# Two attention stages of an encoder kernel: issue order of the score passes, of the value products, and a wider key product

## The chip, the cores and the metric

The kernel runs on one core of a Trainium2 chip. The metric is the device time of one execution in microseconds, from the first to the last instruction. Three executions of the kernel before took 863.78, 861.42 and 863.94 us, median 863.78 us.

## The reference, cut to what matters

A two-layer encoder with 256 tokens and 1024 features, batch one. Layer 0 mixes tokens with a long convolution on 512 channels beside a latent attention of 8 heads; layer 1 mixes them with a differential attention of 8 heads. Each layer then has a cross-attention into 256 memory tokens and a squared-ReLU MLP. The parts that the change touches:

```python
# latent attention, layer 0: 8 heads, 64 plain + 32 rotary key features, 64 value features
kv = (rms_norm(ckv, kv_norm) @ w_ukv).reshape(B, S, 8, 64 + 64)
k_nope, vv = jnp.split(kv, [64], axis=-1)
kf = concat([k_nope, broadcast(k_pe)], axis=-1)              # 96 features per head
o_mla = softmax(qf @ kf.T * 96 ** -0.5) @ vv                 # per head

# differential attention, layer 1: 16 maps of 64 features, two per head
p = softmax(q @ k.T * 64 ** -0.5).reshape(B, 8, 2, 256, 256)
o = (p[:, :, 0] - lam * p[:, :, 1]) @ v                      # per head
```

## The kernel before, in words

All activations of the 256 tokens stay in SBUF as two tiles of 128 tokens; weights stream in through one DMA queue (SP), 512 KB at a time, in the order of issue. Where full precision is wanted, each operand is split into a high and a low part of type fp32r (ScalarE rounds the high part at L105 or L100, VectorE subtracts for the low part at L106 or L101), and a product is three matmuls into one PSUM place: high times high, high times low, low times high. That is the helper `mm3`; its three matmuls have lines L110, L111 and L112, whoever calls it, so the profile tells its callers apart by the tiles. Other products, those of the latent attention's scores (L562) and values (L570) among them, are plain fp32 matmuls; the trace shows each of these as two passes, which is why 16 value products have 32 rows.

PSUM has three pools of banks: four of tag `h`, three of tag `b` (`wk()`), one of tag `f`. Working tiles of 512 columns in SBUF have the tag `t2`, with four buffers in layer 0. The profile leaves the numbers of buffers and parameters out: `b`, `t`, `qkT` and `in_hy_w_dram` stand for all of their kind.

The stages are issued in an order written out by hand (`ORDER_EVEN`, `ORDER_ODD`), as source code. The framework's planner then settles, at build time, the order of instructions on each engine: it takes instructions that its own estimate finds ready, earlier source first, and hands a buffer to a tile when one is free. So an instruction whose PSUM bank is not free is passed by later ones, and the order on the chip is not that of the source. On the chip each engine then follows its own list, and waits where an operand is late.

The places that the change touches:

- `keys_values` (L532 to L545). The weight `w_ukv` has, per head, 64 columns for keys and then 64 for values. For each pair of heads one `b` bank is taken, and each head's keys are one `mm3` with 64 stationary columns, so the result sits on partitions 0 to 63, 256 columns per head: 8 heads make 24 matmuls of 256 columns. ScalarE copies each pair out in one copy of 64 x 512 (L539). The values of all heads are one `mm3` per token tile, which reads every second block of 64 columns of the weight.
- `mla_out` and `mla_o` (L565 to L583). For one head the softmaxed scores are transposed (L426), copied to SBUF (L428) and multiplied by the values (L570): two matmuls of 64 stationary columns and 256 moving columns, accumulated over the two key tiles. An even head writes partitions 0 to 63 of a bank, the odd head after it partitions 64 to 127 of the same bank; the bank is taken at the even head and held until the odd head is done, when L105 and L106 split it into `catm`.
- `od_a` (L798 to L822). A head of the differential attention has two maps. Their queries and keys sit on partitions 0 to 63 and 64 to 127 of one tile, so each score product uses 64 rows of the array. For each of two query tiles and each map there is one `mm3`; the two maps write two `b` banks. In the source all three passes of map 0 come ahead of the three of map 1, and then the second query tile follows in the same way.
- `_layout` (L957) hands `w_ukv` over as it is.

The order of the layer-0 stages around them: queries (U), keys and values (K), transposed queries (R), scores and softmax of head n (Sn), value products of head n (On), chunks of the convolution's input projection (Hn), filters (Fn, whose second weight is loaded into a `t2` tile at L350), and the two spectra (P0, P1), long chains of VectorE work.

Of the kernel before, what the change touches and what calls it, by code (L numbers as in the profile page):

```python
# [17 lines left out]
P = 128  # L18
# [9 lines left out]
PI_LO = 3.1415925  # L28
# Order in which the stages are issued: a letter names the stage (see the run() calls), digits are its arguments.
ORDER_EVEN = "N G J L H0 U K R S0 D H1 F0 S1 T0 S2 S3 P0 O0 O1 O2 H2 S4 O3 H3 T1 F1 S5 S6 O4 O5 Y S7 H4 P1 H5 O6 O7 M W"  # L30
# [8 lines left out]
def tile_encoder(ctx: ExitStack, tc: tile.TileContext, a: dict, out: bass.AP):  # L39
    nc = tc.nc  # L40
# [19 lines left out]
    def wk():  # L60
        return T(ps, [P, 512], F32, "b", bufs=3)
# [10 lines left out]
    def t2(n=512, dt=F32):  # L72
        return T(cur["pool"], [P, 512], dt, "t2", bufs=cur["n2"])[:, :n]
# [10 lines left out]
    def v3(t, k):  # L84
        return t.rearrange("p (k n) -> p k n", k=k)
# [22 lines left out]
    def mm3(o, l, r, first, last):  # L108
        (lh, ll), (rh, rl) = l, r
        nc.tensor.matmul(o, lh, rh, start=first, stop=False)  # L110
        nc.tensor.matmul(o, lh, rl, start=False, stop=False)  # L111
        nc.tensor.matmul(o, ll, rh, start=False, stop=last)  # L112

    def run(order, **ops):
        for w in order.split():
            ops[w[0]](*(int(n) for n in w[1:]))

# [1 line left out]
    es = ExitStack()  # L119
# [43 lines left out]

# [1 line left out]
    def rstd_of(ssq, n, dim, eps):  # L165
# [48 lines left out]

# [1 line left out]
    def proj_x(h, half, k0, nk, n, banks, first, last):  # L216
# [59 lines left out]

# [1 line left out]
    memT = [v3(T(cst, [P, 2048], F32R, f"memT{i}"), 8) for i in range(2)]  # L278
# [21 lines left out]

# [1 line left out]
    def sin_of(b, bias, dst):  # L302
# [96 lines left out]

# [1 line left out]
    def softmax_e(sc, scale=None):  # L401
# [29 lines left out]

    # ======== even mixer ========
    h = v3(t8(F32R), 8), v3(t8(F32R), 8)
# [27 lines left out]
    kT = v3(t8(), 8)  # L461
# [70 lines left out]
    def keys_values():  # L532
        wh, wl = weight(a["w_ukv"])
        for u in range(4):
            b = wk()
            for c in range(2):
                sl = (slice(None), slice((2 * u + c) * P, (2 * u + c) * P + 64))
                mm3(b[:64, c * 256:(c + 1) * 256], (wh[sl], wl[sl]), (latT[0][:, 2, :], latT[1][:, 2, :]), True, True)
            nc.scalar.copy(kT[:64, 2 * u:2 * u + 2, :], v3(b[:64, :], 2))  # L539
        for t in range(2):  # L540
            b = wk()
            sl = (slice(None), 2, slice(t * P, (t + 1) * P))
            wv = [z.rearrange("p (h d) -> p h d", d=P)[:, :, 64:] for z in (wh, wl)]
            mm3(b, (latT[0][sl], latT[1][sl]), wv, True, True)
            nc.scalar.copy(vl[t], b)  # L545
# [18 lines left out]

    def mla_out(hd, e3, ob):  # L565
        pT = v3(t2(), 2)
        transposed(e3, pT)
        r0 = 64 * (hd % 2)
        for m in range(2):
            nc.tensor.matmul(ob[r0:r0 + 64, :256], vl[m][:, hd * 64:(hd + 1) * 64], pT[:, m, :], start=m == 0, stop=m == 1)  # L570

    sc_ = {}
# [4 lines left out]
    def mla_o(hd):  # L577
        if hd % 2 == 0:
            sc_["b"] = wk()
        mla_out(hd, sc_[hd], sc_["b"])  # L580
        if hd % 2:
            split(catm[0][:, hd // 2, :], catm[1][:, hd // 2, :], sc_["b"][:, :256])

# [53 lines left out]

    # ======== cross-attention and MLP ========
    def cross(l, cur_):
# [94 lines left out]

    # ======== odd mixer ========
    os_ = ExitStack()
# [61 lines left out]
    def od_a(hd):  # L798
        j, c = divmod(hd, 4)
        q, k = qkT[0, hd // 2], qkT[1, hd // 2]  # L800
        c %= 2
        av = t2()
        a3 = v3(av, 2)
        es_, su = [], []
        bs = [wk(), wk()]
        for t in range(2):
            for m in range(2):
                rows = slice(64 * m, 64 * m + 64)
                mm3(bs[m][:, t * 256:(t + 1) * 256], [z[rows, c, t * P:(t + 1) * P] for z in q], [z[rows, c, :] for z in k],
                    True, True)  # L810
        for b in bs:
            e3, s_ = softmax_e(b)
            es_.append(e3)
            su.append(s_)
        w = col(2)
        nc.vector.reciprocal(w, su[1])
        nc.vector.scalar_tensor_tensor(w, w, nlam, su[0], op0=ALU.mult, op1=ALU.mult)
        eps = T(op, [P, 2], F32, "eps", bufs=4)
        nc.vector.scalar_tensor_tensor(eps, su[0], SUBLN_EPS, su[0], op0=ALU.mult, op1=ALU.mult)
        for t in range(2):  # L820
            nc.vector.scalar_tensor_tensor(a3[:, t, :], es_[1][:, t, :], w[:, t:t + 1], es_[0][:, t, :],
                                           op0=ALU.mult, op1=ALU.add)  # L822
        st[hd] = a3, eps
# [105 lines left out]
def _layout(i, c):  # L929
# [11 lines left out]
    def both(fn, w):  # L941
# [14 lines left out]
        "w_uq": i["mla_w_uq"][0].reshape(2, P, 768),  # L956
        "w_ukv": i["mla_w_ukv"][0],  # L957
        "w_out_ev": rows(i["ev_w_out"][0]),
# [45 lines left out]
```

## Time and profile before

| | |
|---|---|
| median of three runs | 863.78 us (861.42 to 863.94) |
| profiled execution | 861.42 us, which is its span (861.4 us on the page) |
| TensorE matmul busy | 841.5 us (98%) |
| VectorE / ScalarE busy | 567.4 us (66%) / 482.8 us (56%) |
| DMA | 139.53 MB, mean 162 GB/s |
| score passes of the differential attention (`qkT`) | 96 matmuls, 485.6 to 559.6 us |
| value products of the latent attention (L570) | 32 passes, 67.1 to 122.0 us |
| keys of the latent attention (L110 to L112, `latT` by 64 columns) | 24 matmuls, from 37.4 us |

How to read the views: the page has one execution. A row of the timeline gives the start in us, the duration in us, engine, line, operation, tiles and shapes, how many instructions were merged, and, in brackets, idle time ahead of it with what ended it. The duration of a matmul is its way through the array, and successive matmuls overlap; what one costs is the distance from its start to the next start. "128*64 128x256" means 128 rows and 64 columns of the array in use, 256 columns streamed. The table of windows gives, per stretch, the busy time of each engine with the count of its instructions in brackets, the granted TensorE clock, the DMA share and GB/s.

### The profile page before, as it was taken

How to read it: one execution, taken by the hardware profiler on the slowest of the kernel's cores; microseconds unless marked ns; L12 is line 12 of the kernel's file. 1: busy time of each engine (PE TensorE's matmuls, PEld its weight loads, DVE VectorE, ACT ScalarE, POOL GpSimd, SP SyncE). 2: the span in 40 equal slices, each digit the busy share in tenths (PEclk: the TensorE clock that was granted, in tenths of full speed). 3: DMA queues.
4: the chain of work that ended last, by engine and by line, in shares of the span. 5: the costliest groups of instructions: out<-in, count | busy, mean ns of one | idle time of the engine just before them, and what ended most of it. 6: DMA issues, size and time to landing. Idle time of an engine off the chain costs nothing.

```text
span 861.4 us, 13548 instructions
## 1 busy us (share of the span) xinstructions
PE 841.5 (98%) x5326; PEld 742.0 (86%) x5326; DVE 567.4 (66%) x880; ACT 482.8 (56%) x784; POOL 21.4 (2%) x54
## 2 busy tenths in 40 slices
PE   6999999999999999999999999999999999999996
PEld 4967587999989999999988787789998999999995
DVE  5878986855557655655568889576564765565553
ACT  5864444755447555555467676675443755555542
POOL 0100000000000000000000010200000000000000
PEclk9999999999999999999999999999999999999998
DMA  7550317744344555555536524325432465555531
GB/s 259 201 216 18 118 43 276 259 157 154 117 147 173 195 189 183 191 191 182 191 126 222 171 99 155 139 99 196 149 121 74 167 201 181 187 195 183 185 121 49
DMA packets 39526, 139.53 MB, mean 162 GB/s; under 512 B 4515, under 2 KB 5283, under 8 KB 39462
## 3 DMA queue, kind: packets, MB, share of 16 engines
q1 hardware_dynamic: 39462, 138.66, 46.8%
q8 instruction: 42, 0.69, 0.3%
q14 instruction: 22, 0.18, 0.1%
HBM read 137.59 MB, written 1.05 MB: 161 GB/s over the span
## 4 chain that ended last, share of the span: by engine, by line
PE 86%; issue 7%; DMA 2%; ACT 2%; DVE 1%; POOL 1%; SPq 0%; POOLq 0%; ACTq 0%
PE h L110 14%; PE h L111 14%; PE h L112 14%; PE b L110 11%; PE b L111 10%; PE b L112 10%; PE f L110 2%; PE f L111 2%; PE f L112 2%; PE b L175 1%; DMA t<-in_hy_w_dram 1%; DMA pack<-in_pack_dram 1%; PE b L839 1%; PE b L426 1%; DMA wraw<-in_xa_wk_dram 1%
## 5 line engine op out<-in xcount | busy, mean ns | idle before, releaser
L106 DVE TENSOR_TENSOR wlo<-wraw,whi 128x1024 fp32r<-128x1024 f32 (+2 forms) x131 | 158.5, 1213 | 120.7 <-ACT whi L105 119.9
L105 ACT CAST whi<-wraw 128x1024 fp32r<-128x1024 f32 (+2 forms) x131 | 135.7, 1041 | 146.9 <-PE b L111 58.0
L100 ACT ACTIVATE whi<-wraw,zero,cpack 128x512 fp32r<-128x512 f32 x208 | 159.3, 809 | 66.9 <-PE b L111 33.3
L101 DVE SCALAR_TENSOR_TENSOR wlo<-wraw,cpack,whi 128x512 fp32r<-128x512 f32 x208 | 150.6, 750 | 54.5 <-ACT whi L100 54.2
L110 PE MATMUL b<-t,whi 128*128 128x256 f32 x544 | 154.3, 284 | 0.0
L112 PE MATMUL b<-t,wlo 128*128 128x256 f32 x544 | 154.1, 283 | 0.0
L111 PE MATMUL b<-t,whi 128*128 128x256 f32 x544 | 154.1, 283 | 0.0
L110 PEld LDWEIGHTS b<-t,whi 128*128 128x128 f32 x544 | 104.5, 192 | 0.9 <-issue 0.4
L111 PEld LDWEIGHTS b<-t,whi 128*128 128x128 f32 x544 | 104.5, 192 | 0.5
L112 PEld LDWEIGHTS b<-t,wlo 128*128 128x128 f32 x544 | 104.5, 192 | 0.0
L112 PE MATMUL h<-whi,ul 128*128 128x512 f32 x256 | 100.0, 390 | 0.0
L111 PE MATMUL h<-wlo,uh 128*128 128x512 f32 x256 | 99.9, 390 | 0.0
L110 PE MATMUL h<-whi,uh 128*128 128x512 f32 x256 | 99.9, 390 | 0.0
L110 PE MATMUL h<-whi,t 128*128 128x512 f32 x192 | 77.1, 402 | 0.0
L111 PE MATMUL h<-wlo,t 128*128 128x512 f32 x192 | 76.6, 399 | 0.0
L112 PE MATMUL h<-whi,t 128*128 128x512 f32 x192 | 76.0, 398 | 0.0
L112 PEld LDWEIGHTS h<-whi,ul 128*128 128x128 f32 x256 | 48.1, 188 | 9.9
L110 PE MATMUL h<-t,whi 128*128 128x256 f32 x192 | 55.8, 291 | 0.6 <-ACT t L105 0.6
L110 PEld LDWEIGHTS h<-whi,uh 128*128 128x128 f32 x256 | 48.2, 188 | 9.5
L111 PEld LDWEIGHTS h<-wlo,uh 128*128 128x128 f32 x256 | 48.1, 188 | 9.5
L111 PE MATMUL h<-t,whi 128*128 128x256 f32 x192 | 55.3, 288 | 1.0 <-DVE t L106 1.0
L112 PE MATMUL h<-t,wlo 128*128 128x256 f32 x192 | 55.4, 289 | 0.0
(287 smaller groups left out, 1549.2 us busy)
## 6 DMA issues: line engine op xcount, KB each, us to landing
wraw<-in_mlp_up_dram SPq DMA_DIRECT2D x64, 512.0 KB, 3.3
wraw<-in_mlp_down_dram SPq DMA_DIRECT2D x64, 512.0 KB, 3.2
wraw<-in_od_w_qkv_dram SPq DMA_DIRECT2D x24, 512.0 KB, 4.3
wraw<-in_xa_wq_dram SPq DMA_DIRECT2D x16, 512.0 KB, 4.3
wraw<-in_xa_wo_dram SPq DMA_DIRECT2D x16, 512.0 KB, 3.6
wraw<-in_w_hy_dram SPq DMA_DIRECT2D x12, 512.0 KB, 4.6
wraw<-in_w_out_ev_dram SPq DMA_DIRECT2D x8, 512.0 KB, 4.8
wraw<-in_xa_wv_dram SPq DMA_DIRECT2D x8, 512.0 KB, 4.9
```

Of the source, the lines that this page charges most:

```text
L100: nc.scalar.activation(h_, r_, AF.Identity, bias=zero, scale=g)
L101: nc.vector.scalar_tensor_tensor(l_, r_, g, h_.bitcast(F32), op0=ALU.mult, op1=ALU.subtract)
L105: nc.scalar.copy(hi, src)
L106: nc.vector.tensor_tensor(lo, src, hi.bitcast(F32), op=ALU.subtract)
L110: nc.tensor.matmul(o, lh, rh, start=first, stop=False)
L111: nc.tensor.matmul(o, lh, rl, start=False, stop=False)
L112: nc.tensor.matmul(o, ll, rh, start=False, stop=last)
L175: nc.tensor.transpose(b[:, k * P:(k + 1) * P], x[:, k * P:(k + 1) * P], ident)
L426: nc.tensor.transpose(b3[:, m, t * P:(t + 1) * P], p3[:, t, m * P:(m + 1) * P], ident)
L839: nc.tensor.matmul(ob[:, t * P:(t + 1) * P], aT[:, m, t * P:(t + 1) * P], vo[j][:, m, c * P:(c + 1) * P], start=m == 0, stop=m == 1)
```

## The change

Three edits. The score passes of a head's two maps alternate pass by pass through a new helper `abreast`. The value products of two heads move from the even and the odd head's step to the odd head's step, and alternate between the heads; the even head's transposed block waits in its `t2` tile, and the bank is taken only then. The columns of `w_ukv` are put on the host's side into key columns of all heads, then value columns of all heads, so that keys of two heads are one `mm3` of 128 stationary columns; ScalarE copies each head's keys out by itself, the second head's from partitions 64 to 127 to partitions 0 to 63.

```diff
+    def abreast(jobs):
+        for i, (il, ir) in enumerate(((0, 0), (0, 1), (1, 0))):
+            for o, l, r in jobs:
+                nc.tensor.matmul(o, l[il], r[ir], start=i == 0, stop=i == 2)
...
         for u in range(4):
             b = wk()
+            mm3(b[:, :256], [z[:, u * P:(u + 1) * P] for z in (wh, wl)], [z[:, 2, :] for z in latT], True, True)
             for c in range(2):
-                sl = (slice(None), slice((2 * u + c) * P, (2 * u + c) * P + 64))
-                mm3(b[:64, c * 256:(c + 1) * 256], (wh[sl], wl[sl]), (latT[0][:, 2, :], latT[1][:, 2, :]), True, True)
-            nc.scalar.copy(kT[:64, 2 * u:2 * u + 2, :], v3(b[:64, :], 2))
+                nc.scalar.copy(kT[:64, 2 * u + c, :], b[64 * c:64 * c + 64, :256])
...
-            wv = [z.rearrange("p (h d) -> p h d", d=P)[:, :, 64:] for z in (wh, wl)]
-            mm3(b, (latT[0][sl], latT[1][sl]), wv, True, True)
+            mm3(b, (latT[0][sl], latT[1][sl]), (wh[:, 512:], wl[:, 512:]), True, True)
...
-    def mla_out(hd, e3, ob):
-        pT = v3(t2(), 2)
-        transposed(e3, pT)
-        r0 = 64 * (hd % 2)
-        for m in range(2):
-            nc.tensor.matmul(ob[r0:r0 + 64, :256], vl[m][:, hd * 64:(hd + 1) * 64], pT[:, m, :], start=m == 0, stop=m == 1)
...
     def mla_o(hd):
-        if hd % 2 == 0:
-            sc_["b"] = wk()
-        mla_out(hd, sc_[hd], sc_["b"])
+        pT = v3(t2(), 2)
+        transposed(sc_[hd], pT)
+        sc_[hd] = pT
         if hd % 2:
-            split(catm[0][:, hd // 2, :], catm[1][:, hd // 2, :], sc_["b"][:, :256])
+            ob = wk()
+            for m in range(2):
+                for c in range(2):
+                    h_ = hd - 1 + c
+                    nc.tensor.matmul(ob[64 * c:64 * c + 64, :256], vl[m][:, h_ * 64:(h_ + 1) * 64], sc_[h_][:, m, :],
+                                     start=m == 0, stop=m == 1)
+            split(catm[0][:, hd // 2, :], catm[1][:, hd // 2, :], ob[:, :256])
...
         for t in range(2):
-            for m in range(2):
-                rows = slice(64 * m, 64 * m + 64)
-                mm3(bs[m][:, t * 256:(t + 1) * 256], [z[rows, c, t * P:(t + 1) * P] for z in q], [z[rows, c, :] for z in k],
-                    True, True)
+            abreast([(bs[m][:, t * 256:(t + 1) * 256],
+                      [z[64 * m:64 * m + 64, c, t * P:(t + 1) * P] for z in q],
+                      [z[64 * m:64 * m + 64, c, :] for z in k]) for m in range(2)])
...
-        "w_ukv": i["mla_w_ukv"][0],
+        "w_ukv": i["mla_w_ukv"][0].reshape(P, 8, 2, 64).transpose(0, 2, 1, 3).reshape(P, 1024),
```

## The prediction, made before the run

> **What bounds the kernel now.** I read the page first, then the windows around the three edits, then the timeline of each. The page:
>
> ```profile
> span 861.4 us, 13548 instructions
> ...
> PE 86%; issue 7%; DMA 2%; ACT 2%; DVE 1%; POOL 1%; SPq 0%; POOLq 0%; ACTq 0%
> ```
>
> TensorE makes 86% of the chain that ended last. So time saved on TensorE counts where nothing else is just as late. The windows (keys; the stretch after them; the stretch of the value products, and two further on that come up below):
>
> ```profile
> 37.40:40.30 2.90, 2.90 (x26) 2.71 (x24) 2.50 (x8) 2.90 (x6) 0.00 (x0) 1.00 0.90 285
> 40.30:44.00 3.70, 3.70 (x27) 3.02 (x25) 3.10 (x4) 3.70 (x8) 0.00 (x0) 1.00 0.62 228
> ```
> ```profile
> 66.00:126.00 60.00, 59.59 (x357) 44.59 (x356) 53.11 (x114) 27.27 (x55) 0.74 (x2) 1.00 0.15 49
> 165.00:172.00 7.00, 5.38 (x38) 4.98 (x38) 5.43 (x6) 3.63 (x5) 0.00 (x0) 0.91 0.93 333
> 172.00:180.00 8.00, 8.00 (x61) 8.00 (x60) 2.92 (x3) 3.17 (x4) 0.00 (x0) 0.87 0.52 168
> ```
>
> After the length of the window come TensorE, weight loads, VectorE, ScalarE, GpSimd, the granted TensorE clock, the DMA share. Around the keys ScalarE has no idle time either (2.90 of 2.90 us, 3.70 of 3.70); around the value products VectorE comes second, 53.11 of 60 us.
>
> **Part 1, keys.** It removes 12 of 24 matmuls and replaces four ScalarE copies by eight of half the width.
>
> ```profile
> 37.43 0.28 PE L110 MATMUL b<-latT,whi 128*64 128x256 f32 x1
> 37.55 0.28 PE L111 MATMUL b<-latT,whi 128*64 128x256 f32 x1
> ```
> ```profile
> 38.95 1.54 ACT L539 COPY t<-b 64x512 f32<-64x512 f32 x3
> 40.38 1.06 ACT L105 CAST whi<-wraw 128x1024 fp32r<-128x1024 f32 x1
> 41.34 0.59 ACT L539 COPY t<-b 64x512 f32<-64x512 f32 x1
> ```
> ```profile
> 42.14 1.93 PE b L554 x16
> 44.07 0.23 SPq L142
> 44.30 0.05 issue
> 44.36 7.16 DMA t<-in_hy_w_dram
> 51.51 0.14 issue
> 51.65 3.67 PE h L356 x8
> ```
>
> One matmul of 256 columns costs 0.12 us (37.43 to 37.55), so TensorE saves 12 x 0.12 = 1.4 us. I count it as nothing. ScalarE works without a break from 37.40 to 44.00 (the windows), so its four key copies (1.54 + 0.59 = 2.1 us) and the cast between them set when banks come free for the values and for the transposes L554; eight copies of half the width cost no less. And the chain of waits, the fence above, shows what stands behind: the transposes L554 release a load on SP (L142), the filter weight is issued behind it at 44.36 and lands at 51.51, and L356 starts at 51.65. TensorE arriving earlier waits there longer. The bounds: -1.4 us if ScalarE and the load follow; +2.0 us if each narrow copy takes as long as a wide one (1.54 / 3 = 0.51 us, eight of them 4.1 us) and the load moves back as much. A copy's width must count for something, so I stay between them, at nothing. The values' contiguous read changes no count of columns: nothing.
>
> **Part 2, value products.** The timeline around the first head's, and four other fp32 passes in the chain of waits:
>
> ```profile
> 66.85 0.28 PE L110 MATMUL h<-t,whi 128*128 128x256 f32 x1
> 67.06 1.08 PE L570 MATMUL b<-t,vl 128*64 128x256 f32 x4
> 68.07 0.44 PE L426 MATMUL b<-cpack,t 128*128 128x128 f32 x2
> ```
> ```profile
> 55.32 0.86 PE b L562 x4
> ```
>
> A head's product is four passes, 67.06 to 68.07: 1.01 us. Four plain fp32 passes of 256 columns without such a change of shape cost 0.86 (L562), so 0.15 us of it is extra, and the matmul ahead takes 0.21 (66.85 to 67.06) instead of 0.12: 0.09 more. A visit to the 64-column shape thus costs 0.24 us besides its passes; a head costs 1.10, eight heads 8.8 us.
>
> After the change there are four visits, of eight passes each, and neighbours use the two column halves. Two bounds. No overlap: 4 x (8 x 0.215 + 0.24) = 7.8, a saving of 1.0 us. Full overlap, each half going its own way: 4 x (0.86 + 0.24) = 4.4, a saving of 4.4 us. No row of before has both column halves side by side. The nearest are the two row halves of the score passes:
>
> ```profile
> 523.96 0.39 PE L112 MATMUL h<-whi,t 128*128 128x512 f32 x1
> 524.19 0.40 PE L110 MATMUL h<-whi,t 128*128 128x512 f32 x1
> 524.52 0.38 PE L110 MATMUL b<-qkT,qkT 64*128 64x256 f32 x1
> ...
> 525.09 0.28 PE L111 MATMUL b<-qkT,qkT 64*128 64x256 f32 x2
> 525.21 0.28 PE L112 MATMUL b<-qkT,qkT 64*128 64x256 f32 x2
> ```
>
> There two passes (x2) start every 0.12 us, the time of one, so row halves overlap fully. They also pay the same kind of toll on entering: 0.33 us from 524.19 to 524.52 where the 512-column matmul ahead took 0.23, so 0.10 more, against 0.09 for the value products. That toll shows that the value products already run in a half-array shape; the keys, also 64 columns wide, pay none (37.43 to 37.55), and their halves are never neighbours. So I take the end that these rows are nearest to, full overlap, 4.4 us gross. Were each product's two passes to stay in a row, a pair would need five steps instead of four and 0.9 us of it would be lost; the score passes above, which pair out of source order, speak for four.
>
> How much of it arrives? VectorE is the cover that runs out. Its second spectrum ends just when TensorE wants it:
>
> ```profile
> 101.02 1.02 PE L378 MATMUL h<-z,c_dft 128*128 128x512 f32 x2
> 102.40 1.08 PE L570 MATMUL b<-t,vl 128*64 128x256 f32 x4 [0.35 <-ACT t L428]
> ```
> ```profile
> 119.68 0.68 DVE L397 TENSOR_TENSOR h<-h,h 128x512 f32<-128x512 f32 x1
> ```
> ```profile
> 120.28 0.39 PE L624 MATMUL h<-c_dft,h 128*128 128x128 f32 x2
> ```
>
> L397 is the spectrum's last step, and L624 multiplies its results. The spectrum's inputs leave TensorE with the two L378 at 101.02, ahead of the third pair's products (the first is at 102.40). So what the third pair saves, 1.1 us, would only let L624 wait longer. The first two pairs come ahead of L378, and the last one's second product after L624, so their savings count as long as VectorE, with 60 - 53.1 = 6.9 us to spare in this stretch, keeps up. I keep three quarters: 3.3 us, between 0 (VectorE's slack is all dependent waiting) and 4.4. What the move does to the queues:
>
> ```profile
> SPq L350 <- PE b L570: 12.1, 1, 12.1
> ```
> ```profile
> 72.28 0.33 SPq L350 DMA_DIRECT2D t<-in_hy_w_dram  x1
> ```
> ```profile
> L356 PE MATMUL b<-t,aT x8: 592/592/596, 87.1 to 90.3; 128*128 128x512 f32 x8
> ```
>
> The moved products issue no transfer, but a transfer waits for one of them: SP's load of the second filter weight (L350) stands 12.1 us for a `t2` tile, until an even head's product frees it at 72.28, and its user L356 comes at 87.1, 14.8 us later. Now the even head's block stays until the odd head's product. Other tiles come free meanwhile: two with the first pair's joint product, and the odd head's block can take the tile that its own transposes have just emptied. I count nothing, with 14.8 us of cover; were the load to wait for the second pair's product, it would go out when that is done, about when L356 wants it, and cost its landing, at most the 7.2 us of the first filter weight (44.36 in the chain). The bank is taken later than now: nothing.
>
> **Part 3, score passes.** The order of passes changes, nothing else. In the fence above second passes (L111, 525.09) of two maps start together, then third ones, although the source has all three passes of one map ahead of the other's. The array already pairs what stands in its list triple after triple. Where the two maps stand apart, alternation can't bring them together, since the planner passes by a map whose bank isn't free:
>
> ```profile
> 490.86 0.38 PE L110 MATMUL b<-qkT,qkT 64*128 64x256 f32 x1
> ...
> 491.76 0.50 PE L110 MATMUL h<-whi,t 128*128 128x512 f32 x1
> ```
> ```profile
> 558.93 0.38 PE L110 MATMUL b<-qkT,qkT 64*128 64x256 f32 x1
> ```
>
> These begin the first and the last of eight runs of six passes alone (48 of 96; the rest stand in three visits, that at 524.52 one of them). A run costs 0.90 us (490.86 to 491.76) and the 0.10 ahead of it: 1.0 us. Value taken: nothing. Bounds: four pairs of such runs joined save 4 x 1.0 = 4.0 us; the three joined visits coming apart cost 3 x 1.0 = 3.0.
>
> A rule speaks to this. The Trainium skill, page "TensorE: Matmul & The Clock Gate", section "Part 3: Packing small matmuls — row/col tiling", says that matmuls start and end strictly in program order. By it the source order would pair only neighbouring ends of two triples, and alternation would matter (rival 3). The pair of L111 at 525.09 disagrees with that.
>
> **The sum.** Profiled execution: 861.4 - 0 - 3.3 - 0 = 858.1 us, its span being its whole time. It was the fastest of three; from the median, 863.8 - 3.3 = 860.5 us, my forecast. What may lie between two runs is seen in the windows from 165 to 180 us: behind 7.00 - 5.38 = 1.6 us without matmuls the granted clock fell, and 7 x 0.09 + 8 x 0.13 = 1.7 us were lost. One such dip more or less is most of the spread of 2.5 us.
>
> **Rivals.**
>
> 1. *Column halves don't overlap.* Both write one bank, and no row shows it done; against it stands the toll, equal to the row halves'. Saving 1.0: 862.8 us.
> 2. *The scores come together.* Alternate passes, or the banks' new timing upstream, let the planner place both maps in one visit: 4.0 us more, 856.5 us. For it: three heads already run so. Against it: three `b` banks for two maps and a transposed block.
> 3. *Strict order on the array.* Then alternation saves three steps of 0.12 in each of the heads that now stand in one visit, 3 x 3 x 0.12 = 1.1 us more: 859.4 us. The L111 rows speak against it.
> 4. *Turning between halves pays the toll, the slower side.* Now there are eight visits. If each change of column half empties the array as a change of shape does, two products of two heads make four turns per pair, sixteen in all: 16 x (0.43 + 0.24) = 10.7 us (0.43 for two passes) against 8.8, +1.9: 865.7 us; with a turn at each of 32 passes, 32 x (0.215 + 0.24) = 14.6, +5.8: 869.6 us. It decides from the ninth turn on. Against it: the row halves above change sides within a run without any gap. The Trainium skill, page "TensorEngine Tiling (Array Packing)", section "Tiling Modes", says that changing the mode drains the array and changing the tile does not; by that rule this rival falls, and the row halves agree, while no run here shows column halves.
>
> **How the numbers follow.** Forecast 0.49; rival 1 0.21; rival 2 0.12; rival 3 0.04; rival 4 0.14. The range runs from rival 2's 856.5 to rival 4's first price, 865.7; I set 856.5 to 866. A measurement of this kernel tells about 0.3%, 2.6 us, from no change. Faster by more (below 861.2): two thirds of the forecast, rivals 2 and 3: 0.32 + 0.12 + 0.04 = 0.48. Slower by more (above 866.4): 0.08 from rival 4 and 0.06 from clock dips on top of the others: 0.14. Within: 0.38.
>
> **What would show it.** L570 in four visits of about 1.0 us with starts in pairs shows part 2; visits of 1.9 us show rival 1, more than 2.1 us rival 4. L356 still released by the load near 51.6 us, with more idle time ahead of it, shows part 1. Runs of six `qkT` passes alone, as many as now, show part 3; fewer show rival 2. If L624 doesn't wait, more than 3.3 us arrives. The forecast is wrong if the planner's new order of issue moves the odd layer's visits by more than two.

## The result, and the profile after

The changed kernel takes 868.87 us (median of 5, 864.74 to 871.90), the kernel before, in the same comparison, 862.72 us (861.01 to 863.94). The ratio is 1.0059 (95% interval 1.0032 to 1.0086): slower by about 0.6%, where 860.5 us was forecast and the range ended at 866. The profiled execution after took 865.22 us, its span is 863.2 us: about 2 us lie outside of a span. So the profiled execution before, with its span of 861.4 us, took some 863.4 us (an estimate from these 2 us): it was not the fastest of the three, as the table of before and the prediction have it, but near their median.

The page of the changed kernel:

```profile
span 863.2 us, 13538 instructions
...
PE 91%; DVE 3%; ACT 2%; DMA 2%; issue 1%; POOL 1%; SPq 0%; POOLq 0%; ACTq 0%
```

TensorE still makes most of the chain that ended last. What is new stands in the windows around the edits (columns as in the prediction). Before:

```profile
80.00:95.00 15.00, 15.00 (x66) 8.82 (x65) 11.29 (x27) 6.99 (x14) 0.00 (x0) 1.00 0.23 69
117.00:136.00 19.00, 19.00 (x112) 15.50 (x111) 15.17 (x27) 7.43 (x12) 0.00 (x0) 1.00 0.44 161
160.00:180.00 20.00, 18.38 (x139) 17.98 (x138) 12.72 (x15) 10.38 (x14) 0.00 (x0) 0.91 0.74 254
```

After:

```profile
80.00:95.00 15.00, 12.58 (x54) 7.44 (x53) 11.32 (x28) 6.38 (x13) 0.00 (x0) 0.89 0.25 87
117.00:136.00 19.00, 15.96 (x115) 13.52 (x114) 18.87 (x41) 7.89 (x13) 0.00 (x0) 1.00 0.18 57
...
160.00:180.00 20.00, 20.00 (x167) 19.80 (x167) 14.69 (x18) 12.59 (x17) 0.00 (x0) 1.00 0.84 272
```

TensorE, before without idle time from 80 to 95 and from 117 to 136 us, now loses 15 - 12.58 = 2.4 us in the one window and 19 - 15.96 = 3.0 us in the other, and gains 20 - 18.38 = 1.6 us in the last. Over 60 to 180 us it is idle for 5.8 us instead of 2.9. The waits of TensorE name what ended them (line, releaser, us in all, times, longest); before, then after:

```profile
PE h L111 <- DVE t L106: 1.0, 1, 1.0
PE b L110 <- ACT t L105: 0.9, 1, 0.9
PE h L110 <- ACT t L105: 0.6, 1, 0.6
```
```profile
PE b L582 <- ACT t L433: 2.8, 2, 2.4
PE h L626 <- DVE h L399: 1.6, 1, 1.6
PE h L627 <- DVE h L400: 1.1, 1, 1.1
```

(Lines of the helpers and stages are 2 to 15 higher after: L582 is the value product that was L570, L433 the copy that was L428, L415 the exponential that was L410, L383 was L378, L626 and L627 were L624 and L625.) There are two new waits.

**The stall at 83 us.** ScalarE around the second pair's products, before and then after:

```profile
80.68 1.05 ACT L105 CAST whi<-wraw 128x1024 fp32r<-128x1024 f32 x1 [2.66 <-PE h L111]
...
82.99 0.59 ACT L428 COPY t<-b 128x512 f32<-128x512 f32 x1
...
84.15 1.03 ACT L105 CAST whi<-wraw 128x1024 fp32r<-128x1024 f32 x1
```
```profile
82.84 1.05 ACT L105 CAST whi<-wraw 128x1024 fp32r<-128x1024 f32 x1 [1.83 <-PE h L111]
...
84.25 0.47 ACT L415 ACTIVATE t<-b,col 128x256 f32<-128x256 f32 x1
...
85.15 0.59 ACT L433 COPY t<-b 128x512 f32<-128x512 f32 x1
```

Before, a weight's cast stands behind the copy of the odd head's block. After, a cast stands ahead of the exponentials and the copy, and it waits (1.83 us idle) until TensorE is done with the weight whose buffer it takes over, near 82.8 us. The exponentials and the copy stand behind it in ScalarE's list, and the copy starts 2.2 us later (85.15 instead of 82.99). TensorE has run out of other work by then:

```profile
85.79 1.32 PE L582 MATMUL b<-t,vl 128*64 128x256 f32 x6 [2.42 <-ACT t L433]
...
87.53 1.92 PE L598 MATMUL h<-h,c_dft 128*128 128x512 f32 x2
89.23 1.36 PE L599 MATMUL h<-h,c_dft 128*128 128x512 f32 x2
```

And behind the stall three passes of 512 columns take about twice their time: the two L598 take 1.70 us (87.53 to 89.23), where the prediction's rows give 0.43 for one (L562's four of half the width took 0.86). The window 80 to 95 has a clock of 0.89, which costs 15 x 0.11 = 1.7 us; within it, the clock was 0.50 from 86.5 to 89.9 us.

**The late spectrum.** One of the second pair of matmuls that feed VectorE's second spectrum has slid behind 48 others:

```profile
114.57 1.02 PE L383 MATMUL h<-z,c_dft 128*128 128x512 f32 x2
...
127.62 0.71 PE L626 MATMUL h<-c_dft,h 128*128 128x128 f32 x4 [1.56 <-DVE h L399]
129.43 0.49 PE L627 MATMUL h<-c_dft,h 128*128 128x128 f32 x2 [1.10 <-DVE h L400]
```
```profile
107.00 0.69 DVE L350 TENSOR_TENSOR h<-h,h 128x512 f32<-128x512 f32 x1
...
117.91 0.68 DVE L349 TENSOR_TENSOR h<-h,h 128x512 f32<-128x512 f32 x1
```

Before, both L378 were out by 102 us. Now VectorE's spectrum stands between 107 and 118 us, and TensorE waits 2.7 us for its end.

**The visits.** In the changed kernel, and then the one it should have been four times, as an experiment below shows it:

```profile
67.80 0.65 PE L582 MATMUL b<-t,vl 128*64 128x256 f32 x2
68.38 0.33 PE L431 MATMUL b<-cpack,t 128*128 128x128 f32 x1
68.63 1.08 PE L582 MATMUL b<-t,vl 128*64 128x256 f32 x6
```
```profile
68.68 1.08 PE L582 MATMUL b<-t,vl 128*64 128x256 f32 x8
69.69 0.33 PE L431 MATMUL b<-cpack,t 128*128 128x128 f32 x1
```

There are seven visits and not four: for three of the four pairs the planner issues the even head's first product by itself. From start to the next start they take 0.58, 1.01, 0.58, 1.26 (at the lower clock), 0.58, 1.01 and 1.50 us: 6.5 us, where eight times 1.01 were 8.1 before. So 1.6 us were saved and not 4.4. The column halves do overlap: six passes in 1.01 us are four steps.

### The profile page after: what moved, and what is told of

Read it like the earlier page. It is cut to its first block, busy times and chain, and to the rows that moved or that the text cites. A ratio compares the mean times of both kernels' runs of the same rounds, so it can differ in the third digit from the quotient of the medians.

```text
span 863.2 us, 13538 instructions
## 1 busy us (share of the span) xinstructions
PE 840.2 (97%) x5314; PEld 739.4 (86%) x5314; DVE 568.6 (66%) x880; ACT 484.5 (56%) x788; POOL 19.6 (2%) x54
## 4 chain that ended last, share of the span: by engine, by line
PE 91%; DVE 3%; ACT 2%; DMA 2%; issue 1%; POOL 1%; SPq 0%; POOLq 0%; ACTq 0%
PE h L110 14%; PE h L111 14%; PE h L112 14%; PE b L110 11%; PE b L111 11%; PE b L112 11%; PE f L110 2%; PE f L111 2%; PE f L112 2%; PE b L180 1%; PE b L117 1%; PE b L840 1%; PE b L565 1%; DMA pack<-in_pack_dram 1%; PE b L431 1%
## 5 line engine op out<-in xcount | busy, mean ns | idle before, releaser
L110 PE MATMUL b<-t,whi 128*128 128x256 f32 x544 | 154.6, 284 | 0.0
L111 PE MATMUL b<-t,whi 128*128 128x256 f32 x544 | 153.9, 283 | 0.0
L111 PEld LDWEIGHTS b<-t,whi 128*128 128x128 f32 x544 | 104.4, 192 | 0.8 <-issue 0.2
L110 PEld LDWEIGHTS b<-t,whi 128*128 128x128 f32 x544 | 104.3, 192 | 0.8 <-issue 0.2
L111 PE MATMUL h<-wlo,uh 128*128 128x512 f32 x256 | 99.8, 390 | 0.0
L110 PE MATMUL h<-whi,uh 128*128 128x512 f32 x256 | 99.8, 390 | 0.0
L110 PE MATMUL h<-whi,t 128*128 128x512 f32 x192 | 77.1, 401 | 0.0
L111 PE MATMUL h<-wlo,t 128*128 128x512 f32 x192 | 76.4, 398 | 0.0
L110 PEld LDWEIGHTS h<-whi,uh 128*128 128x128 f32 x256 | 48.1, 188 | 9.5
L111 PEld LDWEIGHTS h<-wlo,uh 128*128 128x128 f32 x256 | 48.1, 188 | 9.5
L110 PE MATMUL h<-t,whi 128*128 128x256 f32 x192 | 55.1, 287 | 0.0
L111 PE MATMUL h<-t,whi 128*128 128x256 f32 x192 | 54.5, 284 | 0.0
```

## Experiments

Four kernels have one part alone, or leave one out. Theory A: the value products lose the time. B: the keys' copies do. C: only the three together come out so badly.

**Values alone** (the edits of `mla_o` put into the kernel before, nothing else):

> The kernel before with the joint value products alone. Theory A (the value products lose the time: the planner issues the even head's first product by itself, and puts the second pair's products ahead of a ScalarE copy that is late): a stall of TensorE of about 2.6 us ahead of the second pair's products, slower passes behind it, the second pair of L378 behind a long run of other matmuls and a wait of TensorE for the second spectrum; in all +2 us in an execution without further clock drops, +4 to +7 us where they come. Theory B (the keys' eight narrow ScalarE copies lose it, and the values only show it later): no such stall, about 3 us faster, as the prediction had it. Theory C (any edit moves the planner's list, and only the three together come out so badly): within 1 us of before.

856.82 us, ratio 0.9939 (0.9925 to 0.9952): faster by 5.3 us. TensorE's row from 60 to 180 us:

```profile
60.00:180.00 120.00, 119.67 (x760) 97.89 (x759) 101.49 (x180) 64.91 (x115) 1.63 (x4) 1.00 0.44 152
```

It is idle for 0.3 us. In ScalarE's list the copy (82.12 us) stands ahead of the cast (83.28), as before the change.

**Keys alone** (the edits of `keys_values` and `_layout`):

> The kernel before with the wide key product alone. Theory A: ScalarE takes about 3 us for eight copies in place of 2.1 us, the transposes L554 end about 1 us later, and of that little stays behind the load of the filter weight: 0 to +1 us. Theory B: +2 to +6 us, with slower passes between 60 and 125 us. Theory C: within 1 us.

859.41 us, 0.9967 (0.9955 to 0.9980): faster by 2.8 us.

```profile
60.00:180.00 120.00, 118.73 (x733) 96.12 (x732) 100.34 (x176) 62.66 (x113) 1.63 (x4) 1.00 0.44 152
```

**Scores alone** (`abreast` in `od_a`):

> The kernel before with the alternating score passes alone. Theories A and B: the row halves overlapped before, the visits of the score passes stay as they are, 0 us (within 0.5). If instead the odd layer loses time (the runs of six come apart into more visits): +1 us for each visit more.

861.86 us, 1.0002 (0.9989 to 1.0015): nothing. Two of the eight runs of six passes come apart here, as in the change (into five and one, and four and two), but they don't cost the 1 us each that was expected.

**Keys and scores, no values:**

> The whole change without its value products (wide keys and alternating scores stay). Theory A: without the value products the change costs 0 to +1 us, and its stall at 83 us and the slower passes at 87 to 90 us are gone. Theory B: it costs as much as the change, +2 to +6 us. Theory C: within 1 us, and nothing to be seen of the stall.

859.85 us, 0.9971 (0.9959 to 0.9982). A and B fall: each of the two parts is faster by itself, and the two together are slower than neither. The instruction lists, as built, say where: with keys and values TensorE's order around the value products is that of the whole change, with values and scores that of the values alone (neither of these two pairs was run). C is too vague to be a cause; so the places are taken one by one. Theory D: the two waits above, both made by the order in the lists. E: the torn visits. F: the eight narrow copies.

**The joint product as a later stage**

```diff
-ORDER_EVEN = "... O0 O1 O2 H2 S4 O3 H3 T1 F1 S5 S6 O4 O5 Y S7 H4 P1 H5 O6 O7 M W"
+ORDER_EVEN = "... O0 O1 X0 O2 H2 S4 O3 H3 T1 F1 Y X1 S5 S6 O4 O5 X2 S7 H4 P1 H5 O6 O7 X3 M W"
```

> The whole change, with the joint product as a stage of its own that is issued later in the source (the second pair's behind the stage Y). ScalarE's list is as in the change: a weight cast L105 still stands ahead of the exponentials and the copy that the second pair waits for. Theory D (two places of the planner's lists lose the time: TensorE's list has the second pair's product where it must wait for that late copy, 2.6 us and some 1.7 us of half clock behind it; and the second L383 pair stands behind 48 matmuls, so that VectorE's second spectrum ends about 10 us late and TensorE waits 3.5 us): here the product stands behind the filter's matmuls, and the L383 pairs ahead of the chunk; both waits are gone: 856 to 858 us. Theory E (torn pairs of visits lose it): one pair stays torn, so at most 1.5 us below the change, 864 to 867 us. Theory F (the eight narrow key copies on ScalarE lose it): as the change, 865 to 869 us.

859.13 us, 0.9970 (0.9960 to 0.9981). The late spectrum is gone, but the stall isn't; another instruction now stands in it:

```profile
84.50 0.49 PE L445 MATMUL h<-cpack,hy 128*128 128x128 f32 x2 [2.03 <-ACT t L415]
```

So the place of the product on TensorE was not the cause: ScalarE is behind by the cast, and whatever TensorE has next waits for it.

**The odd head first in each pair of passes**

```diff
-                for c in range(2):
+                for c in (1, 0):
```

> The whole change with the odd head first in each pair of passes, so that the planner can't issue an even head's pass by itself: four visits of eight passes. In the lists the second pair's product still stands where it waits for the late copy; the L383 pairs stand together ahead of the chunk. Theory D: the stall of about 2.6 us at 83 us stays, with the slower passes behind it; the wait for the second spectrum is gone (3.5 us) and the whole visits save about 1 us: 860 to 864 us. Theory E: everything comes back, about 856 us. Theory F: 865 to 869 us.

857.90 us, 0.9948 (0.9931 to 0.9965): 9 to 11 us below the two medians of the change, from two exchanged loop values. The visits are four of eight passes and 1.01 us each (the fence above), but for the one in the stall:

```profile
84.71 1.98 PE L582 MATMUL b<-t,vl 128*64 128x256 f32 x8 [2.42 <-ACT t L433]
```

The stall stays, as D has it, and the late spectrum is gone; the time lies 2 us below D's band and 2 us above E's. The exchange makes the visits whole and moves the spectrum's input at once, so this run alone can't part the two.

**The key copies on VectorE** (`nc.vector.tensor_copy` for `nc.scalar.copy`):

> The whole change with the eight key copies on VectorE. ScalarE's list then has the cast behind the exponentials and the copy for the second pair, TensorE's list has the pair's product behind the first of the two L598, and the L383 pairs ahead of the chunk. Theory D: no stall near 83 us, no late spectrum, 854 to 857 us. Theory E: two pairs stay torn, 862 to 866 us. Theory F: the 1 us at the transposes and all that follows comes back, 854 to 860 us; so D and F are told apart by the other two.

861.52 us, 0.9993 (0.9979 to 1.0007). Nearest to E, but not by the visits: of the stall 0.5 us are left, but the transposed queries start 3.4 us later than in the change, and TensorE waits near 125 and 168 us again. F gets nothing from it.

**Values alone, odd head first** (the exchange of e6 in e1):

> The kernel before with the joint value products alone, odd head first: four whole visits, no weight cast ahead of the second pair's copy, but the second L378 pair stands behind 48 matmuls, as in the change. Theory D: the late spectrum alone shows: about 3 us over the values alone (856.8), 859 to 861 us. Theory E: whole visits are better than torn ones, 855 to 856.5 us.

859.21 us, 0.9966 (0.9954 to 0.9979): slower than the values alone by 2.4 us, though its visits are whole. This is the late spectrum alone, without the stall; L111 waits again too, 1.0 us at 165 us:

```profile
PE h L624 <- DVE h L395: 1.1, 1, 1.1
...
PE h L623 <- DVE h L394: 0.6, 1, 0.6
```

Next the spectrum is put earlier in the whole change, in two ways. Theory G: before loses 2 us at 168 us to the order of its loads.

```diff
-... O5 Y S7 H4 P1 H5 O6 O7 M W     (the change)
+... O5 Y S7 P1 H4 H5 O6 O7 M W     (first)
+... O5 Y P1 S7 H4 H5 O6 O7 M W     (second)
```

> The whole change with the stage P1 (the second spectrum) ahead of H4 in the written order of layer 0. In the lists the two L383 pairs then stand ahead of the 96 matmuls; the cast ahead of the second pair's copy stays, the visits of the value products stay torn, and the order of the loads in the cross-attention stays as in before (a key weight of the second layer, fraw, ahead of the two value weights). Theory D (late cast and late spectrum): TensorE's waits of 1.7 and 1.3 us for the second spectrum are gone, the stall of 2.6 us at 83 us stays, and the end of the output projection comes 4 to 6 us earlier. Theory G (in before, TensorE waits 2 us at 168 us for loads, because fraw stands ahead of the value weights; the change hid it only by being late): that wait comes back, about 2 us and its half clock. Together 861 to 865 us. Without G: 859 to 861 us.

861.21 us, 0.9999 (0.9985 to 1.0013).

```profile
PE b L582 <- ACT t L433: 2.4, 1, 2.4
PE h L111 <- DVE t L106: 1.0, 1, 1.0
PE h L110 <- ACT t L105: 0.7, 1, 0.7
```

The waits for the spectrum are gone, the stall stayed, and the two waits of before near 168 us came back, as D and G together have it: 6 to 8 us below the change.

> As the run before this one, but P1 stands ahead of S7 too, and this puts both value weights of the cross-attention ahead of fraw in the list of loads. Theories D and G: no wait for the spectrum, none for loads at 168 us; the stall at 83 us stays: 858 to 861 us, 2 to 4 us below the run before. Without G: no difference between the two.

861.31 us, 0.9999 (0.9984 to 1.0015): no better, and a wait of 1.2 us at 170 us, though the value weights were loaded first. That speaks against G, and so does the next.

**Before, with the cross-attention's value weights ahead**

```diff
-    "V0 K0 Q0 K1 S0 V1 B0 ...
+    "V0 K0 Q0 V1 K1 S0 B0 ...
```

> The kernel before with nothing but the cross-attention's second value stage (V1) ahead of the second key stage (K1) in the written order of layer 0's cross-attention; the lists of everything earlier are as before. The value weights are then loaded ahead of fraw. Theory G: the waits at 168 us (0.8 and 1.3 us above the pace, and 1.7 us of lower clock behind them) are gone: 858 to 860 us, and then some 3 us of what the keys alone (859.4) and the values alone (856.8) had gained came from the order of these loads and not from their own work. Without G: 862 us, as before.

863.04 us, 1.0004 (0.9992 to 1.0017): nothing.

```profile
PE b L110 <- ACT t L105: 1.1, 1, 1.1
PE h L111 <- DVE t L106: 1.0, 1, 1.0
```

One of the three waits of before, that of 0.6 us, is gone (it shrinks to 0.2 us in e3 too, which leaves these loads as they are); the other two are not. G as written falls. Its core stays: L110 and L111 wait there for the two halves of an activation's split, which stand on ScalarE and VectorE behind the splits of weights. In the lists of all kernels with this wait, three loads of the second layer's key weight go out early. Of the kernels with two such loads (e1, e2, e4, e6, e14, e15, e17, e18) none has it; of those with three, only e5 and one execution of the change don't. The two go together; that the third load makes the wait is not shown.

**Values, odd head first, and P1 ahead of H4:**

> Joint value products alone (no wide keys, no alternating scores), odd head first, and P1 ahead of H4. In the lists: four whole visits, the L378 pairs ahead of the 96 matmuls, no weight cast ahead of the second pair's copy, the value weights ahead of fraw. Theories D and G: no stall at 83 us, no late spectrum, no wait at 168 us, and a visit less in three pairs: 855 to 856.5 us, below the values alone (856.8). Theory E (torn visits are the loss): the same. Theory that only chance moves the planner's lists: anywhere from 856 to 862 us.

858.66 us, 0.9953 (0.9938 to 0.9969). The spectrum is early, the visits whole, but TensorE waits 2.0 us near 164 us: another list with three early loads.

Now the cast itself is moved away from the copy, by one exchange in the written order of the whole change:

```diff
-... O2 H2 S4 O3 H3 ...
+... O2 H2 O3 S4 H3 ...
```

> The whole change; the only other edit is that O3 stands ahead of S4 in the written order of layer 0. In ScalarE's list the second pair's copy then stands directly behind one weight cast and ahead of the cast that waited for its buffer, TensorE's list has the pair's products inside the chunk H3, and the L383 pairs stand ahead of the 96 matmuls. The visits stay torn and the key copies stay. Theory D: the stall of 2.6 us at 83 us goes, the half clock behind it goes, the late spectrum goes: from the change's 865.2 (its profiled execution) 2.6 + 1.7 + 3.5 = 7.8 us less, 857 to 859 us, up to 3 us more if TensorE then waits for a weight's split near 168 us as it does in before. If the keys' copies or the torn visits were the loss: 864 to 869 us.

864.37 us, 1.0028 (1.0014 to 1.0041): 4.5 us below the change and 2.8 below its repeat beside it (867.12, further down), but 2 above the end of what D allowed. TensorE's waits:

```profile
PE h L180 <- DVE t L277: 2.5, 1, 2.5
PE h L445 <- DVE hy L511: 1.1, 2, 0.7
PE h L111 <- DVE t L106: 1.0, 1, 1.0
```

L582 doesn't wait, but L445 does, 1.1 us near 86 us. The late spectrum is gone too, and the other waits are elsewhere, most of them between 125 and 172 us, where the DMA share is 0.7 to 0.8: four loads of the output projection now stand behind the norm's, ahead of all that the cross-attention loads. (The next run has the same four, with 47 - 45.71 = 1.3 us idle in that stretch instead of 47 - 42.32 = 4.7, so they alone don't make these waits.)

**The same, odd head first:**

> The whole change, O3 ahead of S4 as in the run before, and the odd head first in each pair of value passes: four whole visits, the copy ahead of the cast, the L383 pairs ahead of the 96 matmuls, two instead of three early loads of the second layer's key weight. Theory D: odd head first (857.9) less its stall of 2.6 us: 854 to 856 us, with visits of about 1.0 us; below both kernels.

858.01 us, 0.9952 (0.9936 to 0.9969): as e6, not below it.

**Both passes of the even head, then both of the odd** (the loops over `c` and `m` exchanged in the values alone):

> The kernel before with joint value products in which both passes of the even head stand ahead of both of the odd head (no alternation). If the array starts a later pass ahead of its turn in the list when its half is free, whole visits take 1.0 us, as alternated ones with the odd head first. If only neighbours in the list overlap: one pair at the border of the heads, 7 steps of 0.215 and 0.15 more, about 1.66 us.

857.50 us in one execution. ScalarE's two copies and a first visit of eight passes:

```profile
66.61 1.08 ACT L428 COPY t<-b 128x512 f32<-128x512 f32 x2
```
```profile
67.26 1.56 PE L579 MATMUL b<-t,vl 128*64 128x256 f32 x8
68.75 0.44 PE L426 MATMUL b<-cpack,t 128*128 128x128 f32 x2
```

1.49 us (67.26 to 68.75), between the two expectations, and the reason is not the order of the passes: the even head's block is ready 0.49 us ahead of the odd head's, whose copy ends at 67.69 (66.61 + 1.08). The odd head's first pass starts at 67.746, just behind that, beside the even head's third (67.742) and ahead of its fourth (67.958), and its four passes take 1.01 us. So 0.49 and 1.01 make up the visit, and the halves overlap here too, also where the list has head after head. What such a list takes with both blocks ready isn't shown: in each of this kernel's whole visits the odd head's block was late. The values alone, alternated but with the even head first, take the same 1.50 (67.40 to 68.90), for the same reason: the copies end at 67.35 and 67.84, so the even head's first product is done alone. With the odd head first nothing starts until both are there, and all four pairs form.

**The change once more:**

> The changed kernel once more, beside the others. Theory D: 865 to 870 us; its stall at 83 us and its waits near 125 us are there in each execution, and what differs between executions is how long the lower clock behind them lasts: a longer execution shows more stretches of 0.85 us per pass of 512 columns where 0.43 is the pace.

867.12 us, 1.0049 (1.0030 to 1.0067), five executions of 865.29 to 867.82. The profiled one (867.82, span 865.9) and the first one (span 863.2) differ from 165 us on; the window of this one (the first one had no idle time there, and a clock of 1.00):

```profile
165.00:180.00 15.00, 13.11 (x96) 12.71 (x95) 8.93 (x11) 7.06 (x9) 0.00 (x0) 0.89 0.82 288
```

The wait of before near 168 us comes back in this execution (L110 and L111, 0.9 and 1.0 us): 1.9 us of idle time and 15 x 0.11 = 1.7 us of lower clock, more than the 2.7 us between the spans. D's expectation, that longer executions show more of the lower clock, held, though it had not foreseen the wait ahead of it. It holds for the others too: the mean granted clock of the change's ten executions goes from 0.996 in the shortest (864.74 us) to 0.989 in the longest (871.90 us).

**Values, odd head first, O3 and P1 moved.** Two last orders, chosen in the lists by four marks: whole visits, the copy ahead of the last cast, both L378 pairs ahead of the 96 matmuls, two early loads and not three.

```diff
-... O0 O1 O2 H2 S4 O3 H3 T1 F1 S5 S6 O4 O5 Y S7 H4 P1 H5 ...
+... O0 O1 O2 H2 O3 S4 H3 T1 F1 S5 S6 O4 O5 Y S7 P1 H4 H5 ...     (e17)
+... O0 O1 O2 O3 H2 S4 H3 T1 F1 S5 S6 O4 O5 Y S7 P1 H4 H5 ...     (e18)
```

> Joint value products alone, odd head first, O3 ahead of S4 and P1 ahead of H4. In the lists: four whole visits, the second pair's copy ahead of the last weight cast, the L378 pairs ahead of the 96 matmuls, two early loads of the second layer's key weight and not three. Theory D (what decides is how long TensorE waits in the first 180 us): the matmuls alone take as little as with the odd head first (165 us up to the second key block of the cross-attention, beside 167.5 for the values alone), and the waits are as few as with the values alone (about 2 us): 853 to 855 us. If each such order only moves the waits elsewhere (as in the runs with P1 or O3 moved): 857 to 860 us.

855.90 us, 0.9921 (0.9899 to 0.9944).

> As the run before, but O3 stands ahead of H2, so that the first two pairs' products come close together ahead of the chunk. Lists as good by the same three marks: 853 to 855 us by theory D, 857 to 860 us if the waits only move.

855.42 us, 0.9920 (0.9901 to 0.9939): the fastest, 6.5 us below before and 13 below the change.

```profile
67.77 1.08 PE L579 MATMUL b<-t,vl 128*64 128x256 f32 x8
70.66 1.08 PE L579 MATMUL b<-t,vl 128*64 128x256 f32 x8
...
101.06 1.08 PE L579 MATMUL b<-t,vl 128*64 128x256 f32 x8 [0.67 <-ACT t L428]
...
117.38 1.08 PE L579 MATMUL b<-t,vl 128*64 128x256 f32 x8
```
```profile
60.00:180.00 120.00, 118.96 (x773) 99.34 (x772) 101.83 (x181) 65.91 (x118) 1.63 (x4) 1.00 0.44 152
```

Four whole visits, and only 1.0 us idle. So the saving can arrive; the waits need not merely move. Both runs lie just above D's 853 to 855 us, and below the 857 to 860 of waits that only move.

All in one table. The idle time is 120 us less TensorE's busy time from 60 to 180 us in the profiled execution, with the clock there:

| kernel | median us | ratio | idle us, clock |
|---|---|---|---|
| before | 861.8 to 862.7 | | 2.9, 0.99 |
| the change; again (e16) | 868.87; 867.12 | 1.0059; 1.0049 | 5.8, 0.99; 7.4, 0.97 |
| values (e1); one head after the other (e15) | 856.82; 857.50 | 0.9939; one run | 0.3; 0.4, 1.00 |
| keys (e2); keys and scores (e4) | 859.41; 859.85 | 0.9967; 0.9971 | 1.3; 1.3, 1.00 |
| scores (e3); loads moved (e11) | 861.86; 863.04 | 1.0002; 1.0004 | 2.8; 2.5, 1.00 |
| values, odd first (e8); with P1 (e12) | 859.21; 858.66 | 0.9966; 0.9953 | 3.2; 2.5, 1.00 |
| change, odd first (e6); with O3 (e14) | 857.90; 858.01 | 0.9948; 0.9952 | 2.9, 0.99; 3.4, 1.00 |
| change, later stage (e5) | 859.13 | 0.9970 | 2.3, 1.00 |
| change, P1 moved (e9; e10) | 861.21; 861.31 | 0.9999; 0.9999 | 4.3, 0.97; 3.9, 0.99 |
| change, O3 moved (e13) | 864.37 | 1.0028 | 6.4, 1.00 |
| change, copies on VectorE (e7) | 861.52 | 0.9993 | 4.2, 1.00 |
| values, odd first, O3 and P1 (e17; e18) | 855.90; 855.42 | 0.9921; 0.9920 | 0.8; 1.0, 1.00 |

## Why the prediction was wrong

**Which step failed.** "How much of it arrives?" The prediction asked what might swallow a saving of 4.4 us, set the bounds at 0 and 4.4, and kept 3.3. It had no bound below nothing: it took the lists around the products as they were and priced only the matmuls. But the planner makes its lists anew, and TensorE's idle time between 60 and 180 us went from 2.9 to 5.8 us, in another execution to 7.4. Of the profiled pair, 2.9 us more idle time less the 1.6 us saved in the visits is 1.3 us, beside 1.8 us between the spans (863.2 and 861.4), each with one stretch of half clock between 60 and 180 us. In e16, 4.5 us more idle time and one more such stretch of 1.7 us, less 1.6, are 4.6 us, beside 4.5 us between the spans (865.9 and 861.4). Neither of the two new waits is among the rivals. Of the 0.14 for slower, 0.08 stood for rival 4, which fell; the other 0.06, for clock dips, has a part of what happened, but not the waits that the dips followed. And the sign that was to show the planner's new order, the odd layer's visits, was the wrong place to look: two runs came apart there at no cost, and the loss is in layer 0.

**Part 2, overlap: right in kind, wrong in size.** The starts are in pairs, 6 to 7 ns apart, and a whole visit takes 1.01 us (e6, e18), as "four visits of about 1.0 us" has it. The rival that turning between halves pays is refuted, and the rival of no overlap. The Trainium skill, page "TensorEngine Tiling (Array Packing)", section "Tiling Modes", says that changing the tile within one mode doesn't drain the array; e6 agrees with it. The mis-sized term is the 4.4 us: in the change as written it is 1.6, because three visits are torn (0.58 us for the even head's first product alone), and in the fourth the even head's block is ready 0.49 us ahead of the odd head's. Whole visits can be had by two exchanged loop values. The Trainium skill, page "TensorE: Matmul & The Clock Gate", section "Part 3: Packing small matmuls — row/col tiling", says that matmuls start in program order. The L111 of the prediction's score rows disagree with it; e15 decides nothing here, since its products (67.26, 67.742, 67.746 and 68.23 us) start in the list's order and only the two passes within them don't.

**Part 2, cover: wrong.** That VectorE "keeps up" failed, but not for VectorE's speed: the last L383, its input, left TensorE at 114.57 instead of 101.02 us, behind 48 more matmuls. The named sign, L624 (now L626), waited, which it had not done before. There the prediction also read a row wrongly: it took the spectrum to end just when TensorE wants it, by L397, but what L626 waits for is L399, which is L394 of before,

```profile
117.87 0.68 DVE L394 TENSOR_TENSOR h<-h,h 128x512 f32<-128x512 f32 x1
```

and that is done at 118.55, 1.7 us ahead of L624 at 120.28. The second filter weight was rightly priced at nothing, but narrowly: it went out 11 us later and landed at 86.91 us, ahead of its use at 90.43, and 0.2 us ahead of the 87.1 of before.

**Part 1, keys: right at its place, not in all.** ScalarE's eight copies:

```profile
38.76 3.06 ACT L543 COPY t<-b 64x256 f32<-64x256 f32 x8
```
```profile
45.52 6.15 DMA t<-in_hy_w_dram
...
51.81 1.53 PE h L361 x3
```

They take 0.38 us each, 0.9 us more than four wide ones. The load goes out 1.2 us later for it (45.52 instead of 44.36), but lands only 0.2 us later, since it takes 6.15 instead of 7.16 us: L361 starts at 51.81 us instead of 51.65. That is no chance of one execution: it starts between 51.1 and 52.5 us in all ten profiles with eight ScalarE copies, and between 51.1 and 52.7 in the nine of kernels with four. Why the later load is quicker was not looked into. Yet the keys alone were 2.8 us faster; 2.9 - 1.3 = 1.6 us of that is idle time between 60 and 180 us, above all the wait at 168 us, which their lists had lost. Had only keys been tried, all of it would have been put down to fewer matmuls.

**Part 3, scores: right.** e3 shows nothing gained or lost. Rival 3's 1.1 us did not come: in the change one of the three joined visits has eight passes in 0.67 us instead of 0.79, and the other two take 1.51 and 1.61 us as before.

**The clock.** The prediction read the waits and the lower clock of before at 165 to 180 us as what differs between executions. For the clock that is right: e3 and e11 have these waits too, with a clock of 1.00, and the executions of before at a mean clock of 0.995 or 0.996 took 862.5 to 865.4 us, those at 0.997 or more 860.4 to 863.0. The waits themselves are part of that kernel's lists, 1.6 us idle in its profile, and e1, e2 and e6 don't have them. In the change, that wait comes and goes with the execution (e16). About half of the change's loss is lower clock too: span times mean clock, an estimate of the span at full clock, is 859.7 us (mean of five) and 860.1 (e16), beside 857.5 to 857.9 for before in the five later comparisons, so some 2 to 2.5 of the 5 to 6 us would be left at full clock.

**What stays open.** Why the planner, with both edits, puts the cast ahead of the copy is argued from the lists only: with the wide keys one more weight load of the convolution goes out early, and with the joint products the softmax's work is held to be later. That moving O3 takes the stall away is shown (e13, e14). The longest executions of the change (869 to 872 us) were not profiled: that their clock is lower (0.989 to 0.993) is on record, not which waits stand ahead of it.

## What to carry to other kernels

Where a planner makes the order, price an edit by the lists that come out, not by the instructions that it takes away: an edit can be faster by 5 us, another by 3, and the two together slower. Ask of each engine's list what now stands ahead of the work that the bound engine needs next; here a conversion that waited for its buffer made a copy 2.2 us late. Products meant to share the array are best written so that the one that is ready last stands first (here that made all four visits whole), and a gain seen in a whole-kernel time should be looked for at the place of the edit before it is believed.

## What the runs showed of the hardware

- Column halves of the array run side by side, also for fp32 products of two passes: eight passes of 256 columns in 1.01 us, with starts 6 to 7 ns apart.
- Behind the TensorE stall of 2.4 us near 83 us the granted clock fell in all five profiles that have it (the change twice, e6, e9, e10: 0.97 over 60 to 125 us, passes up to twice as long); behind the 2.0 us of e5 it stayed at 1.00. The length alone doesn't decide: it also stayed at 1.00 behind 2.5 us in e13 (L180, from 142 us), and fell behind two waits of 0.6 and 1.0 us in before.
- Eight ScalarE copies of 64 x 256 took 3.06 us, 0.38 each, beside 0.51 for 64 x 512: here half the width cost three quarters.
